# A hybrid decoder block on one core: the compression weights streamed as high and low halves, the gates' high and low columns held as one operand, and the order of all instructions set by a fixed table of urgencies

## The chip, the cores and the metric

The kernel runs on one core of one Trainium2 chip. The metric is device time in microseconds (us) for one execution, from the first to the last instruction of the program and what lies around it. The kernel before took 537.15 us, the median of three runs between 537.08 and 537.4 us.

## What is computed

One block of a decoder: x has 256 rows of 1,024 columns, and there are 256 memory rows. After an RMS norm, one wide projection `z = h @ w_in` feeds three token mixers (block-sparse attention, an mLSTM, attention to the memory), which are gated, projected, merged and normed, and a SwiGLU channel mixer ends the block. All is in float32. The change touches two small pieces of it, the compression of keys and values and the projection of the gates:

```python
def compress_blocks(kv, pe, w1, w2):
    n_cmp = (S - CMP_BLOCK) // CMP_STRIDE + 1                      # 15 blocks of 32 rows, one every 16
    idx = jnp.arange(n_cmp)[:, None] * CMP_STRIDE + jnp.arange(CMP_BLOCK)[None, :]
    blocks = kv[:, idx] + pe[None, None, :, None, :]
    hid = jax.nn.silu(jnp.einsum('bnlgd,ldh->bngh', blocks, w1))   # w1: 32 x 64 x 128, 4 groups g
    return jnp.einsum('bngh,hd->bngd', hid, w2)

z = h @ w_in[l]                                                    # 48 NSA gates and 8 mLSTM gates are columns of z
gb = jax.nn.sigmoid(g_nsa.reshape(B, S, NSA_GROUPS, NSA_HPG, 3))
gates = if_ml.astype(jnp.float32) + ml_gate_b[l].astype(jnp.float32)
logf = jax.nn.log_sigmoid(gates[..., ML_HEADS:])
```

Compression runs twice, for keys (j = 0) and for values (j = 1); its result feeds the attention scores of the first mixer.

## The kernel before

A float32 product is made of three products of a faster kind. `split` makes of a tile a high part (a rounding copy on ScalarE, type float32r) and a low part (what is left, a subtraction on VectorE), and `mm3` adds high by high, high by low and low by high in PSUM. Weights come in units of 512 KB: `fetch` loads one into `raw` (four buffers), `room` gives it a `whi` and a `wlo` (four each), and two splits fill them. `fmaj` holds weights (128x128 pieces of whi or wlo) and streams the 256 tokens; `tmaj` holds tokens and streams 512 weight columns; `fcat`, late in the kernel, holds weights and streams high and low tokens as 512 columns side by side. The tokens of the first norm are `hh` (high) and `hl` (low), 8 steps k of 128 features.

The stretch that the change touches comes early. First come the keys of the memory (`mem_k`, 96 matmuls named pd) and its values (`mem_v`, 48 matmuls named pss of 512 columns), while VectorE scales the tokens (`xt`) and makes hh and hl. `rstd_bc` works out a row's 1/rms with a power on GpSimd (`rr` for the tokens, `rm` for the memory rows) and spreads it over the partitions with two small matmuls (`rbc`). Then four units `kv` give the keys and values that are to be compressed. For each j, four ScalarE copies set up `st` (64 of 128 partitions), two VectorE copies shift it to the other 64, three GpSimd instructions clear and fill its columns for the position embedding, and 16 plain float32 matmuls hold the 128x128 pieces of `w1` and stream 80 columns of st into `ph`. Column 64 is the embedding's part and becomes the bias of the Silu that writes `hid`. The gates (`pgf`) go through `split` and `fmaj` as a unit padded to 128 columns: 24 matmuls of 256 columns. `pg` transposes them.

The order of the work is not the order of the code. Every call is recorded as an operation (Plan.record), `Plan.choose` finds an order and `Plan.issue` issues it, so that all instructions bear one line (L627). `schedule` gives each engine, in turn, the ready operation with the smallest urgency (a latest start from `latest`, less a boost), by a table of costs. `choose` tries four settings, keeps the best, and then makes 100 random trials: it raises the boost of operations in a chain that TensorE waited for, and keeps what is not longer in its own reckoning (`replay`). All engines work their queues in order; SyncE issues all loads, and a load whose buffer is still read holds up those behind it.

## Time and profile before

| what | value |
|---|---|
| median of three runs | 537.15 us |
| profiled execution, its own time | 536.95 us |
| its span, first to last instruction | 535.2 us |
| TensorE clock granted, mean | 0.996 |
| TensorE (PE) busy | 525.0 us, 3116 records |
| VectorE (DVE) busy | 411.9 us |
| ScalarE (ACT) busy | 342.2 us |
| GpSimd (POOL) busy | 30.8 us |

A busy PE is not PE at its peak: records of matmuls overlap, and a matmul's record (280 ns for 256 columns) is longer than the distance to the next start. So work on PE is counted here from start to start. A plain float32 matmul leaves two records. "Idle before" is time in which an engine had nothing running, with what ended it.

### The profile page before, as it was taken

To read this page: it belongs to the slowest core of one execution; us is meant where nothing else is said; L and a number is where in the kernel's file an instruction comes from. 1 tells how busy PE (TensorE), PEld (TensorE's weight loads), DVE (VectorE), ACT (ScalarE), POOL (GpSimd) and SP (SyncE) were. 2 spreads that over 40 slices of the span, in tenths; PEclk is the share of its full clock that TensorE was granted. 3 is DMA by queue.
4 is the path that set the end of the run, shared out by engine and by line. 5 is a ranking of instruction groups with operands and counts; after the bars stand their busy time and mean duration, and the time that the engine had idled before them with its cause. 6 is when DMAs were issued, how large, how long until landed. Compare 5 with 4: busy or idle time off the path is not lost.

```text
span 535.2 us, 8817 instructions
## 1 busy us (share of the span) xinstructions
PE 525.0 (98%) x3116; PEld 462.3 (86%) x3116; DVE 411.9 (77%) x900; ACT 342.2 (64%) x682; POOL 30.8 (6%) x43
## 2 busy tenths in 40 slices
PE   8999999999999999999999999999999999999995
PEld 8889998998989899888888888788888888888883
DVE  5786598799999988987978897966777777754543
ACT  7686787576699785966895346754665555653431
POOL 0110000020010111120220000000000000000000
PEclk9999999999999999999999999999999999999998
DMA  8995356525524454344465575734555555555512
GB/s 311 417 374 197 130 183 184 193 81 196 198 81 140 137 199 154 108 155 172 159 196 166 184 232 190 252 119 157 188 187 186 191 193 197 198 194 191 187 57 78
DMA packets 28699, 97.85 MB, mean 183 GB/s; under 512 B 3312, under 2 KB 5232, under 8 KB 28400
## 3 DMA queue, kind: packets, MB, share of 16 engines
q1 hardware_dynamic: 28656, 97.30, 52.9%
q8 instruction: 24, 0.39, 0.3%
q14 instruction: 19, 0.16, 0.1%
HBM read 95.19 MB, written 1.05 MB: 180 GB/s over the span
## 4 chain that ended last, share of the span: by engine, by line
PE 87%; DVE 5%; DMA 4%; ACT 1%; issue 1%; POOL 0%; SPq 0%; DVEq 0%; ACTq 0%
PE pd L627 47%; PE pss L627 28%; DMA raw<-in_W 4%; PE pvn L627 3%; PE sc L627 2%; PE ptn L627 2%; PE ph L627 1%; DVE wlo L627 1%; ACT whi L627 1%; DVE xt L627 1%; PE pn L627 1%; PE pvm L627 1%; PE pgf L627 1%; PE psm L627 1%; PE pq L627 1%
## 5 line engine op out<-in xcount | busy, mean ns | idle before, releaser
L627 DVE TENSOR_TENSOR wlo<-raw,whi 128x1024 fp32r<-128x1024 f32 (+1 forms) x159 | 191.8, 1213 | 80.4 <-ACT whi L627 79.9
L627 ACT ACTIVATE whi<-raw 128x1024 fp32r<-128x1024 f32 (+1 forms) x159 | 166.2, 1052 | 116.4 <-PE pd L627 57.2
L627 PE MATMUL pd<-hh,wlo 128*128 128x256 f32 x208 | 58.5, 281 | 0.0
L627 PE MATMUL pd<-hh,whi 128*128 128x256 f32 x208 | 58.4, 281 | 0.0
L627 PE MATMUL pd<-hl,whi 128*128 128x256 f32 x208 | 58.2, 280 | 0.0
L627 PE MATMUL pd<-whi,hh 128*128 128x512 f32 x144 | 57.5, 399 | 0.0
L627 PE MATMUL pd<-wlo,hh 128*128 128x512 f32 x144 | 57.5, 399 | 0.0
L627 PE MATMUL pd<-whi,hl 128*128 128x512 f32 x144 | 56.8, 398 | 0.0
L627 PE MATMUL pss<-xc,whi 128*128 128x512 f32 x168 | 43.1, 392 | 0.0
L627 PE MATMUL pss<-whi,u 128*128 128x512 f32 x132 | 42.0, 390 | 0.0
L627 PEld LDWEIGHTS pd<-hl,whi 128*128 128x128 f32 x208 | 39.3, 189 | 0.2
L627 PEld LDWEIGHTS pd<-hh,whi 128*128 128x128 f32 x208 | 39.2, 188 | 0.2
L627 PEld LDWEIGHTS pd<-hh,wlo 128*128 128x128 f32 x208 | 39.1, 188 | 0.1
L627 PEld LDWEIGHTS pss<-xc,whi 128*128 128x128 f32 x168 | 30.5, 188 | 5.2
L627 PE MATMUL pd<-xc,whi 128*128 128x512 f32 x120 | 31.9, 394 | 0.0
L627 DVE CUSTOM_DVE_ANT_0 sc<-sc,msk 128x16 f32<-128x16 f32 (+2 forms) x96 | 27.2, 313 | 5.2 <-PE sc L627 4.5
L627 PEld LDWEIGHTS pd<-whi,hh 128*128 128x128 f32 x144 | 27.1, 188 | 4.5 <-ACT cx L627 0.2
L627 PEld LDWEIGHTS pd<-whi,hl 128*128 128x128 f32 x144 | 27.1, 188 | 4.5
L627 PEld LDWEIGHTS pd<-wlo,hh 128*128 128x128 f32 x144 | 27.1, 188 | 4.0
L627 PEld LDWEIGHTS pss<-whi,u 128*128 128x128 f32 x132 | 24.8, 188 | 5.2
L627 ACT ACTIVATE pp<-sc,mx 128x128 f32<-128x128 f32 (+1 forms) x64 | 26.9, 434 | 1.8 <-DVE mx L627 1.7
L627 PE MATMUL pss<-wlo,u 128*128 128x512 f32 x66 | 25.7, 389 | 0.0
(335 smaller groups left out, 1123.3 us busy)
## 6 DMA issues: line engine op xcount, KB each, us to landing
raw<-in_W SPq DMA_DIRECT2D x161, 512.0 KB, 3.7
w<-in_w SPq DMA_DIRECT2D x2, 1024.0 KB, 7.5
xn<-in_xN SPq DMA_DIRECT2D x2, 512.0 KB, 9.4
xt<-in_xT SPq DMA_DIRECT2D x2, 512.0 KB, 9.1
mn<-in_memN SPq DMA_DIRECT2D x2, 512.0 KB, 9.3
kk<-kk SPq DMA_DIRECT2D x8, 128.0 KB, 2.8
x<-in_xN SPq DMA_DIRECT2D x2, 512.0 KB, 4.2
memt<-in_head SPq DMA_DIRECT2D x1, 512.0 KB, 7.6
```

The lines of the kernel that those rows point to most:

```text
L627: op.ins_ = getattr(op.real, op.method)(*map(arg, op.a), **{k: arg(x) for k, x in op.kw.items()})
```

## The change

- **Compression.** `st` now holds, for each of 16 steps, the high and the low parts of 64 token columns as one 128x128 held operand (column 63 is the position embedding). `w1` is split as the other weights are, high and low side by side in `w1s` (names wc in the code), and 256 columns of it are streamed: 16 float32r matmuls into `ph` [128, 2, 128] for each j. A ScalarE copy and a VectorE addition join the two halves of the columns (`hs`), one plain float32 matmul with a constant `fold` (`phT`) adds the high rows, the low rows and the embedding's rows, and Silu reads that. The GpSimd instructions for st, the shifting copies of 64 partitions and the bias are gone. ScalarE and VectorE write the two halves of st from PSUM (four each for each j), and VectorE makes the shifted half with one copy of 128 partitions.
- **Gates.** 64 gate columns are loaded, not 128; their high and low parts stand side by side in `gw`, 128 columns that are held as one operand, and high and low tokens (`hx`, one tile with hh and hl in it) are streamed as 512 columns: 8 matmuls. A copy and two additions (`gfold`) join the parts.
- **Order.** The random trials are gone. A table EARLY gives 141 of the operations a boost, in ns, by number; some costs of loads are changed, and the load of w1 stands behind the kv units in the code.

The same program text otherwise makes the instructions: all bear L621 now.

```diff
@@ -230,6 +229,9 @@
         for other in after:
             op.deps.setdefault(other, False)
         op.cost = self.cost(op)
+        if op.dma:
+            self.dmas += 1
+            op.cost *= 1.25 if self.dmas <= 6 else 1.0
...
     NEXT = {"PE": 200.0, "ACT": 135.0, "DVE": 118.0, "POOL": 80.0, "SP": 60.0}
-    START, TABLE, ISSUE, LAND = 570.0, 1283.0, 460.0, 1850.0
+    START, TABLE, ISSUE, LAND, FEED = 570.0, 1283.0, 460.0, 2100.0, 740.0
...
-        free = {e: self.START for e in self.ORDER}
+        free = {e: self.FEED if e == "SP" else self.START for e in self.ORDER}
...
-    MATMUL, SLACK, PASSES, ROUNDS = (-3.0, 0.0), (60.0, 130.0), 3, 100
+    MATMUL, SLACK, PASSES = (-3.0, 0.0), (60.0, 130.0), 3
+
+    EARLY = """
+    2:12586700 3:2093350 4:2092250 5:2093900 83:200700 145:4150 149:1400 150:4700 151:3150 152:7300 153:8600
...
+    """
 
     def choose(self):
 
@@ -554,37 +573,12 @@
         for op, op.rank in zip(self.ops, kept):
             pass
         length, matmul, slack, boost = best
-        rng = random.Random(0)
-        stale = True
-        for _ in range(self.ROUNDS):
-            if stale:
-                order = self.schedule(matmul, slack, boost)
-                self.replay(order)
-                waits = [(op.lost, op) for op in order if op.eng == "PE" and op.lost > 90 and op.why]
-                chains = []
-                for lost, op in waits:
-                    chain, d = [], op.why
-                    while d is not None and len(chain) < 16:
-                        chain.append(d.i)
...
-            if not waits:
-                break
-            chain = rng.choices(chains, [w[0] for w in waits])[0]
-            step = rng.choice((200, 500, 1000, 2000, 4000))
-            new = dict(boost)
-            for i in chain[:rng.choice((1, 2, 4, 8, 16))]:
-                new[i] = new.get(i, 0) + step
-            trial = self.replay(self.schedule(matmul, slack, new))
-            if trial <= length:
-                length, boost, stale = trial, new, True
+        boost = {int(i): int(ns) for i, ns in (x.split(":") for x in self.EARLY.split())}
         self.chosen = length, matmul, slack, boost
         return self.schedule(matmul, slack, boost)
 
     FIRST_BYTE = 0x4080
-    RESIDUE = {"vcs": 0, "V": 0, "C": 0, "G": 0, "qs": 0, "KK": 0xC0, "E": 0xC0, "Y": 0xC0, "hh": 0xC0, "hl": 0xC0,
+    RESIDUE = {"vcs": 0, "V": 0, "C": 0, "G": 0, "qs": 0, "KK": 0xC0, "E": 0xC0, "Y": 0xC0, "hh": 0xC0,
                "whi": 0, "wlo": 0, "raw": 0, "pT0": 0xC0, "pT1": 0xC0, "ce0": 0xC0, "ce1": 0xC0}
 
...
@@ -791,8 +785,8 @@
     mh = bigt("G", 3, [P, KD, S], F32R, "mh")
     ml = bigt("G", 3, [P, KD, S], F32R, "ml")
     xt = bigt("E", 2, [P, KD, S], F32, "xt")
-    hh = bigt("hh", 1, [P, KD, S], F32R, "hh")
-    hl = bigt("hl", 1, [P, KD, S], F32R, "hl")
+    hx = bigt("hh", 1, [P, 2, KD, S], F32R, "hh")
+    hh, hl = hx[:, 0], hx[:, 1]
     X, M = (hh, hl), (mh, ml)
...
-    wgt = work.tile([P, 1024], F32, tag="p", bufs=2, name="wgt")
-    w2t = work.tile([P, 192], F32, tag="ce0", bufs=1, name="w2t")
+    wgt = work.tile([P, KD, 64], F32, tag="p", bufs=2, name="wgt")
+    w2t = work.tile([P, 256], F32, tag="ce0", bufs=1, name="w2t")
...
@@ -884,13 +878,14 @@
                                      op0=ALU.mult, op1=ALU.subtract)
     fetch(("kv", 0))
     fetch(("kv", 1))
-    dma(out=wgt, in_=wg)
+    dma(out=wgt, in_=wg.rearrange("p (k n) -> p k n", k=KD))
     msk = one.tile([P, K_END - K_M0], F32, name="msk")
     w1t = [bigt("G", 3, [P, 16, P], F32, f"w1_{j}") for j in range(2)]
+    fold = w2t[:, 192:256]
     w1_in = lambda j: dma(out=w1t[j], in_=w1[j].rearrange("p (a n) -> p a n", a=16))
-    w1_in(0)
     fetch(("kv", 2))
     fetch(("kv", 3))
+    w1_in(0)
     w1_in(1)
...
@@ -907,39 +902,34 @@
 
     hid = work.tile([P, 2, NG, 32], F32, tag="ce1", bufs=1, name="hid")
     POOL.memset(hid, 0.0)
+    sts = []
     for j in range(2):
 
 
-        st = bigt("E", 2, [P, 16, 96], F32, f"st{j}")
-        POOL.memset(st[:, :, 64:96], 0.0)
-        POOL.memset(st[64:128, 15, 0:64], 0.0)
-        POOL.tensor_copy(st[:, 0:16:2, 64:66],
-                         vc[:, V_PEK + 16 * j:V_PEK + 16 * j + 16].rearrange("p (n l) -> p l n", n=2))
+        st = bigt("E", 2, [P, 2, 8, 2, 64], F32R, f"st{j}")
         ps = fpair(X, "kv", j, (ps_s, ps_d)[j])
+        by_block = lambda t: t.rearrange("p i (n q r) -> p r q i n", n=16, r=2)
         for e in range(2):
-            for i in range(2):
-                g = 2 * i + e
-                ACT.activation(st[0:64, :, 16 * g:16 * g + 16],
-                               ps[64 * e:64 * e + 64, i].rearrange("p (n l) -> p l n", n=16), AF.Copy)
-        DVE.tensor_copy(st[64:128, 0:15, 0:64], st[0:64, 1:16, 0:64])
-        DVE.tensor_copy(st[64:128, 15, 0:63], st[0:64, 0, 1:64])
-
-        ph = ps_v([P, 80], "ph")
-        for l in range(16):
-            n = l // 8
-            PE.matmul(ph, w1t[j][:, l, :], st[:, 2 * l % 16, n:n + 80], start=(l == 0), stop=(l == 15))
-        bias = work.tile([P, 1], F32, tag="b1", bufs=1, name="cbias")
-        DVE.tensor_copy(bias, ph[:, 64:65])
-        ACT.activation(hid[:, j, :, 0:NCMP], ph[:, 0:64].rearrange("p (g n) -> p g n", g=NG)[:, :, 0:NCMP], AF.Silu,
-                       bias=bias)
-
-
-    pgf = ps_s([P, S], "pgf")
-    gw = room()
-    split(gw[0], gw[1], wgt)
-    fmaj(pgf, X, range(KD), gw)
-    gts = work.tile([64, S], F32, tag="sq", bufs=3, name="gts")
-    DVE.tensor_copy(gts, pgf[0:64])
+            for r in range(2):
+                to = st[64 * r:64 * r + 64, 0].rearrange("p q x (i e n) -> p x e q i n", i=2, e=2)
+                split(to[:, 0, e], to[:, 1, e], by_block(ps[64 * e:64 * e + 64])[:, r])
+        DVE.tensor_copy(st[:, 1, :, :, 0:63], st[:, 0, :, :, 1:64].bitcast(F32))
+        pe = vc[:, V_PEK + 16 * j:V_PEK + 16 * j + 16].rearrange("p (h q) -> p h q", h=2)
+        DVE.tensor_copy(st[:, :, :, 0, 63], pe)
+        DVE.tensor_sub(st[:, :, :, 1, 63], pe, st[:, :, :, 0, 63].bitcast(F32))
+
+        sts.append(st)
+
+    pgf = ps_s([P, 2, S], "pgf")
+    gw = wpool.tile([P, 1088], F32R, tag="whi", bufs=4, name="gw")[:, 48:1072].rearrange("p (k i n) -> p k i n", k=KD, i=2)
+    split(gw[:, :, 0, :], gw[:, :, 1, :], wgt)
+    for k in range(KD):
+        PE.matmul(pgf, gw[:, k], hx[:, :, k, :], start=k == 0, stop=k == KD - 1)
+    gfold = work.tile([64, 2, S], F32, tag="sq", bufs=3, name="gfold")
+    gts = gfold[:, 0, :]
+    ACT.activation(gfold, pgf[64:128], AF.Copy)
+    DVE.tensor_add(gfold, gfold, pgf[0:64])
+    DVE.tensor_add(gts, gts, gfold[:, 1, :])
     pg = ps_s([P, 2, 64], "pg")
     for tb in range(2):
         PE.transpose(pg[:, tb, :], gts[:, tb * P:(tb + 1) * P], cs[0:64, K_ID:K_ID + 64])
@@ -957,6 +947,22 @@
     ACT.activation(lf, ef, AF.Ln, bias=1.0)
     logf = one.tile([P, 2, 4], F32, name="logf")
     DVE.scalar_tensor_tensor(logf, f, 0.0, lf, op0=ALU.min, op1=ALU.subtract)
+
+
+    for j in range(2):
+        wc = [bigt(tg, n, [P, 8, 2, P], F32R, "w1s") for tg, n in (("C", 1), ("G", 3))]
+        for h in range(2):
+            split(wc[h][:, :, 0, :], wc[h][:, :, 1, :], w1t[j][:, 8 * h:8 * h + 8, :])
+        ph = ps_v([P, 2, P], "ph")
+        for l in range(16):
+            PE.matmul(ph, sts[j][:, l // 8, l % 8].rearrange("p x n -> p (x n)"), wc[l // 8][:, l % 8],
+                      start=(l == 0), stop=(l == 15))
+        hs = work.tile([P, P], F32, tag="sq", bufs=3, name="hs")
+        ACT.activation(hs, ph[:, 1], AF.Copy)
+        DVE.tensor_add(hs, hs, ph[:, 0])
+        pc_ = ps_t([P, 64], "phT")
+        PE.matmul(pc_, hs, fold, start=True, stop=True)
+        ACT.activation(hid[:, j, :, 0:NCMP], pc_.rearrange("p (g n) -> p g n", g=NG)[:, :, 0:NCMP], AF.Silu)
...
-    yh = bigt("hh", 1, [P, 8, S], F32R, "yh")
-    yl = bigt("hl", 1, [P, 8, S], F32R, "yl")
+    yx = bigt("hh", 1, [P, 2, 8, S], F32R, "yh")
+    yh, yl = yx[:, 0], yx[:, 1]
...
-    w2 = np.concatenate([w2k, w2k, a["cmp_w2_v"][0]], axis=1)
+    fold = np.tile(np.eye(64, dtype=np.float32), (2, 1))
+    fold[63::64] = 1.0
+    w2 = np.concatenate([w2k, w2k, a["cmp_w2_v"][0], fold], axis=1)
     row = np.concatenate([a[n] for n in ("ml_head_g", "ml_gate_b", "g_post_mix", "g_post_ffn", "g_pre_ffn")], axis=1)
-    wg = np.zeros((D, P), np.float32)
+    wg = np.zeros((D, 64), np.float32)
     wg[:, 0:48] = w_in[:, C_G:C_G + 48]
     wg[:, 48:56] = w_in[:, C_IF:C_IF + 8]
-    wg = blocks(wg, slice(None)).reshape(P, 1024)
+    wg = blocks(wg, slice(None)).reshape(P, 512)
 
     cst = np.zeros((P, K_END), np.float32)
     i = np.arange(P)

```

The first 117 instructions on PE and the last 275 are the same as before, apart from names. Three places in the order, before and after, follow.

On GpSimd, from the power for the tokens' norm (rr) to what follows the power for the memory's norm (rm); before:

```order
L627 TENSOR_TENSOR rr<-rv,mhalf 128x2
L627 MEMSET st_381 128x16x32
L627 MEMSET st_381 64x64
L627 COPY st_381<-vc_358 128x8x2
L627 MEMSET st_495 128x16x32
L627 MEMSET st_495 64x64
L627 COPY st_495<-vc_358 128x8x2
L627 TENSOR_TENSOR rm<-rv,mhalf 128x2
```

And in the change:

```order
L621 TENSOR_TENSOR rr<-rv,mhalf 128x2
L621 TENSOR_TENSOR rm<-rv,mhalf 128x2
L621 MEMSET cm_799 4x128
L621 MEMSET cm_834 4x128
L621 MEMSET cx 128x2x3
```

The six instructions that set up st stood between the two powers; nothing stands there now.

On TensorE, the compression of the values before (j = 1; the rows pd around it are units of other projections, st_495 its tokens, w_1_629 its weights):

```order
L627 MATMUL pd<-hh,whi 128x256
L627 MATMUL pd<-hl,whi 128x256
L627 MATMUL ph<-st_495,w_1_629 128x80 x16
L627 MATMUL pg<-cs,gts 128x64 x2
L627 MATMUL pd<-hh,wlo 128x256
```

And the compression of the keys in the change (st_565; the name hh now stands for high and low tokens alike, since they are one tile):

```order
L621 MATMUL pd<-hh,whi 128x256
L621 MATMUL ph<-w1s,st_565 128x256 x8
L621 MATMUL pd<-hh,whi 128x256
L621 MATMUL ph<-w1s,st_565 128x256 x4
L621 MATMUL pg<-cs,gfold 128x64 x2
L621 MATMUL ph<-w1s,st_565 128x256 x4
L621 MATMUL psm<-kmem,qm_731 128x256 x4
```

The 16 matmuls are no longer one block, and the transposes of the gates stand among them; 49 matmuls of projections stand between pgf and the first ph now, where 11 to 12 stood on either side of pgf before.

On VectorE, the rows before from the split of the gate weights to the gates' copy:

```order
L627 TENSOR_TENSOR wlo<-wgt,whi 128x1024
L627 COPY st_381<-st_381 64x63
L627 TENSOR_TENSOR wlo<-raw,whi 128x1024 x2
L627 COPY cbias<-ph 128x1
L627 COPY st_495<-st_495 64x15x64
L627 COPY gts<-pgf 64x256
```

And in the change from the last projection unit ahead of the splits of w1 to the second pair of them:

```order
L621 TENSOR_TENSOR wlo<-raw,whi 128x1024
L621 TENSOR_TENSOR st_637<-pd,st_637 64x8x2x16 x4
L621 TENSOR_TENSOR gfold<-gfold,pgf 64x512
L621 CAST st_637<-st_637 128x16x63
L621 TENSOR_TENSOR w1s<-w_0_580,w1s 128x8x128 x2
L621 TENSOR_TENSOR gfold<-gfold 64x256
L621 CAST st_637<-vc 128x16
L621 TENSOR_TENSOR wlo<-raw,whi 128x1024
L621 TENSOR_TENSOR st_637<-vc,st_637 128x16
L621 TENSOR_TENSOR wlo<-raw,whi 128x1024
L621 TENSOR_TENSOR hs<-hs,ph 128x128
L621 TENSOR_TENSOR w1s<-w_1_647,w1s 128x8x128 x2
```

The subtractions for st and for w1 stand among the low parts of the weight units (wlo) on which the projections' matmuls wait.

More of the change, by code (lines that the diff above doesn't have):

```diff
@@ L2 @@
 import math
-import random
 from contextlib import ExitStack, contextmanager
@@ L176, in __init__ @@
         nc = tc.nc
-        self.tc, self.ops, self.tiles, self.boost = tc, [], {}, 0
+        self.tc, self.ops, self.tiles, self.boost, self.dmas = tc, [], {}, 0, 0
         self.engines = {n: Engine(self, n, e) for n, e in
@@ L471, in replay @@
     def replay(self, order):
-        free = {e: self.START for e in self.ORDER}
+        free = {e: self.FEED if e == "SP" else self.START for e in self.ORDER}
         place, port, busy, done = {}, {}, {}, {}
@@ L556, in choose @@
         length, matmul, slack, boost = best
-        rng = random.Random(0)
-        stale = True
-        for _ in range(self.ROUNDS):
-            if stale:
-                order = self.schedule(matmul, slack, boost)
-                self.replay(order)
-                waits = [(op.lost, op) for op in order if op.eng == "PE" and op.lost > 90 and op.why]
-                chains = []
-                for lost, op in waits:
-                    chain, d = [], op.why
-                    while d is not None and len(chain) < 16:
-                        chain.append(d.i)
-                        d = d.why or max((x for x, strict in d.deps.items() if strict), key=lambda x: x.end,
-                                         default=None)
-                    chains.append(chain)
-                stale = False
-            if not waits:
-                break
-            chain = rng.choices(chains, [w[0] for w in waits])[0]
-            step = rng.choice((200, 500, 1000, 2000, 4000))
-            new = dict(boost)
-            for i in chain[:rng.choice((1, 2, 4, 8, 16))]:
-                new[i] = new.get(i, 0) + step
-            trial = self.replay(self.schedule(matmul, slack, new))
-            if trial <= length:
-                length, boost, stale = trial, new, True
+        boost = {int(i): int(ns) for i, ns in (x.split(":") for x in self.EARLY.split())}
         self.chosen = length, matmul, slack, boost
```

13 rows, old and new, of the table EARLY are left out of this document.

## Prediction

> **What bounds the kernel now.** I read first the page's busy times, then who waited for whom, then the timeline of each engine in the stretch of the change, then the sums by stretch.
>
> ```profile
> PE 525.0 (98%) x3116; PEld 462.3 (86%) x3116; DVE 411.9 (77%) x900; ACT 342.2 (64%) x682; POOL 30.8 (6%) x43
> PE rbc L627 <- POOL rm L627: 1.3, 1, 1.3
> PE warm L627 <- POOL mhalf L627: 1.0, 1, 1.0
> PE pd L627 <- ACT whi L627: 0.8, 1, 0.8
> PE pss L627 <- ACT xc L627: 0.2, 1, 0.2
> ```
>
> TensorE is busy 98% of the span and waits 3.3 us in all, so the span is the sum of its matmuls, a start and a tail. The reader should see two things. First, whatever shortens TensorE's own work shortens the kernel by as much, provided nobody else comes late. Second, one wait, 1.3 us for GpSimd's `rm`, lies in the stretch of the change. So the question has two halves: how much TensorE work goes, and whether VectorE, which takes over work, can keep up.
>
> ```profile
> 30.00:40.00 10.00, 8.70 (x74) 8.50 (x73) 7.77 (x13) 7.38 (x14) 2.48 (x4) 1.00 0.94 356
> 40.00:45.00 5.00, 5.00 (x46) 5.00 (x45) 4.91 (x6) 3.56 (x5) 0.87 (x2) 1.00 0.54 200
> 45.00:60.00 15.00, 15.00 (x133) 14.85 (x132) 5.08 (x13) 10.06 (x15) 0.00 (x0) 1.00 0.48 165
> 60.00:65.00 5.00, 5.00 (x47) 5.00 (x46) 3.86 (x7) 3.96 (x6) 0.00 (x0) 1.00 0.28 101
> 65.00:80.00 15.00, 15.00 (x133) 14.82 (x132) 14.89 (x38) 11.71 (x27) 0.00 (x0) 1.00 0.56 188
> ```
>
> The columns are PE, PEld, DVE, ACT and POOL busy. VectorE has room from 45 to 60 us (5.08 of 15 busy) and none from 65 to 80 (14.89 of 15); TensorE nevertheless did not wait there, because what it ran was ready earlier.
>
> **The compression's matmuls.** These rows are TensorE's timeline; work is counted from start to start.
>
> ```profile
> 36.61 0.28 PE L627 MATMUL pd<-hh,whi 128*128 128x256 f32 x1
> 40.74 0.28 PE L627 MATMUL pd<-hh,wlo 128*128 128x256 f32 x1
> 40.86 3.69 PE L627 MATMUL ph<-st,w 128*128 128x80 f32 x32
> 44.34 0.36 PE L627 MATMUL pd<-hh,whi 128*128 128x256 f32 x1
> 45.80 0.28 PE L627 MATMUL pgf<-hh,whi 128*128 128x256 f32 x1
> 48.52 0.28 PE L627 MATMUL pd<-hh,whi 128*128 128x256 f32 x1
> 49.77 3.69 PE L627 MATMUL ph<-st,w 128*128 128x80 f32 x32
> 53.39 0.33 PE L627 MATMUL pg<-cs,gts 64*128 64x64 f32 x2
> 77.08 1.00 PE L627 MATMUL pvc<-w2t,hrep 128*128 128x64 f32 x8
> 77.92 0.61 PE L627 MATMUL ptx<-cs,pp 128*128 128x128 f32 x4
> ```
>
> The two blocks ph took 44.34 - 40.86 = 3.48 and 53.39 - 49.77 = 3.62 us: 7.10 us go. What comes is 32 float32r matmuls of 256 columns. Such matmuls run at 0.118 us each (35 steps from 36.61 to 40.74) or at 0.113 (pgf: 24 from 45.80 to 48.52). I take 0.113 here and a term for the slower pace below: 32 x 0.113 = 3.62. The two plain float32 fold matmuls of 64 columns cost what a pvc does, (77.92 - 77.08) / 4 = 0.21: 0.42. Net: -7.10 + 3.62 + 0.42 = **-3.06 us**.
>
> **The gates.** 24 matmuls took 48.52 - 45.80 = 2.72 us. For 8 of 512 columns the nearest rows are those of the memory's values:
>
> ```profile
> 17.81 0.40 PE L627 MATMUL pss<-wlo,mh 128*128 128x512 f32 x1
> 20.10 0.39 PE L627 MATMUL pss<-whi,ml 128*128 128x512 f32 x1
> ```
>
> Ten steps in 2.29 us are 0.229 each, so 8 cost 1.83: **-0.89 us**. The new operand streams two pieces of 256 columns that lie apart, where these rows stream one piece; I see no row for that and allow 0 to 0.3 us, taking 0. [...]
>
> **The wait for rm.** These rows are the powers and their neighbours on GpSimd, then VectorE, then TensorE around the wait.
>
> ```profile
> 18.95 0.20 POOL L627 COPY st<-vc 128x16 f32<-128x16 f32 x1 [0.24 <-DMA vc<-in_vec]
> 30.57 0.73 POOL L627 MEMSET st<- 128x512 f32 x2 [11.42 <-DVE hl L627]
> 31.37 1.15 POOL L627 COPY st<-vc 128x16 f32<-128x16 f32 x1
> 32.48 0.69 POOL L627 TENSOR_TENSOR rm<-rv,mhalf 128x2 f32<-128x2 f32 x1
> 30.43 0.16 DVE L627 TENSOR_SCALAR rv<-sums 128x2 f32<-128x2 f32 x1
> 31.24 1.23 DVE L627 TENSOR_TENSOR wlo<-raw,whi 128x1024 fp32r<-128x1024 f32 x1 [0.65 <-ACT whi L627]
> 31.65 0.28 PE L627 MATMUL pss<-hh,wlo 128*128 128x256 f32 x1
> 33.23 0.49 PE L627 MATMUL rbc<-cs,rm 128*128 128x128 f32 x2 [1.30 <-POOL rm L627]
> ```
>
> The sums for rm were ready at 30.59 (30.43 + 0.16). GpSimd, in its queue's order, was still to clear and fill st1, whose buffer came free only with the last hl; the power ran from 32.48 to 33.17, and rbc started at 33.23, where without a wait it would have started at 31.65 + 0.12 = 31.77. That is 1.46 us. The change takes these three instructions out of the queue: the power can start right after its sums and, with its own 0.69 us, end at about 31.3 on before's clock, ahead of the 31.77 at which TensorE wants it. **-1.46 us**; nothing later in GpSimd's queue is due soon. What would be late next is VectorE's wlo of the following unit, below.
>
> **A slower pace.** In this trace the 256-column matmuls ran at 0.118 us before the first ph and at 0.113 after it. I don't know what sets it. If taking the plain float32 block away leaves the slow pace until 78 us, some 200 matmuls lose 0.005 each: 1.0 us. The small float32 matmuls (pg, phT, pf) that stay could end it as well. I take **+0.3**, ends 0 and 1.0.
>
> **VectorE's added work.** Durations by groups:
>
> ```profile
> L627 DVE TENSOR_TENSOR wlo<-raw,whi 128x1024 fp32r<-128x1024 f32 x155 | 189.2, 1226 | 79.4 <-ACT whi L627 78.9
> L627 DVE TENSOR_TENSOR hl<-xt,hh 128x256 fp32r<-128x256 f32 x8 | 2.9, 418 | 0.0
> L627 DVE TENSOR_TENSOR kt<-pd,rmb 128x512 f32<-128x512 f32 x2 | 1.4, 684 | 0.0
> L627 DVE COPY st<-st 64x960 f32<-64x960 f32 x2 | 1.4, 684 | 2.2 <-ACT st L627 2.2
> L627 DVE TENSOR_SCALAR mx<-mx 128x2 f32<-128x2 f32 x4 | 0.6, 148 | 0.0
> L627 DVE COPY gts<-pgf 64x256 f32<-64x256 f32 x1 | 0.4, 417 | 0.7 <-PE pgf L627 0.7
> ```
>
> Added: four low parts of w1 at 1.23 (4.9); eight low parts of st, 256 wide from PSUM, at 0.42 (3.3); two shifting copies at about 0.7 (1.4); four small ones at 0.15 (0.6); gfold at 0.68 and 0.42 (1.1); hs twice at about 0.3 (0.6); gw, 512 wide, 0.7. Sum 12.6. Removed: the copies of st, two of 0.68 and two of about 0.2 (1.8), wgt's low part (1.2), gts (0.4), two biases (0.3): 3.7. Net +8.9 us. Room for it between 30 and 65 us: 35 less 7.77 + 4.91 + 5.08 + 3.86 = 21.6 busy leaves 13.4 us idle; but TensorE now crosses that stretch 3.06 + 0.89 + 1.46 = 5.4 us sooner, so 8.0 are left. 8.9 against 8.0: 0.9 us too little, in front of a stretch (65 to 80) where VectorE is full. I expect it to show where TensorE reaches small matmuls that hang on VectorE's chain (`pm` behind the running maxima `cm`, the transposes `ptx`): **+0.9 us**, ends 0 (projections run ahead instead, as they did before at 65 to 80) and 2.5. ScalarE's share, some 5 us (four high parts of w1, gw, gfold, hs), fits into 45 to 65, where it was busy 10.06 + 3.96 of 20 us.
>
> **Moved things at nothing.** The tokens' rbc stands 12 matmuls later, and scaling xt and making hh and hl is then done in one run; from there to the first matmul that needs hh are 24 x 0.229 = 5.5 us, while VectorE's 16 instructions of that size (hl: 0.42) make 6.7 us, and the eighth step is needed only 7 x 0.35 = 2.5 us after the first. If that cover fails it costs what is short, up to 1 us. A unit is loaded ahead of the rows for the norms on SyncE's queue; it has the same margin. `hid` is ready later, by a copy, an addition and the fold, but its first reader stands just ahead of pvc, at about 75 us. Elsewhere the order differs in many places, but the waits above leave little to win or lose outside the stretch: 0, ends -0.8 and +0.8.
>
> **The sum.** -3.06 - 0.89 - 1.46 + 0.3 + 0.9 = -4.2 us. The profiled execution took 536.95, so 532.7 there; against the median of 537.15, which stands 0.2 higher, 532.9. That is the forecast.
>
> **The rivals.** (1) The wait for rm stays, behind another lock. The copy of 16 elements took 0.20 us at 18.95 but 1.15 at 31.37, and it ended at 32.52, just after VectorE's subtraction from two SBUF tiles (31.24 to 32.47). If the power comes when such a subtraction is under way, it stands still until that ends: the power is then done as late as before, at 33.17, and the 1.46 us stay: 534.4. In before the sums led the next subtraction by 0.65 us idle, which speaks against; in the change ScalarE's order still puts the unit's high part behind the sums. Chance 0.2. [...]
>
> (2) VectorE becomes the bound. If none of its idle time can be used, because the splits are tied to the arrival of units and to four buffers, all 8.9 us land on TensorE's path: -5.4 + 0.3 + 8.9 = +3.8, that is 541, slower. For it speaks that VectorE is full from 65 to 80; against it that its 10 us of idle time at 45 to 60 lie just where the new work becomes ready. It is slower than before by 0.2% once over 6.2 us stay uncovered. Chance 0.04 for that, and 0.08 for a half of it, which is no change that can be told (-0.6).
>
> (3) All of the new work is covered, the fast pace holds and the new order saves some of the rest: -5.4 - 0.8 gives 530.9. Chance 0.2.
>
> (4) Nothing is won on the matmuls: the new ones run as plain float32 in two passes. The 128-column rows at 77.92 and the block ph show such passes at about 0.11 us per 80 columns, so 32 of 256 columns would take over 10 us more. The operands are float32r like those of pd; chance 0.01.
>
> **How the numbers follow.** The forecast has 0.47. A measurement of this kernel can tell about 0.2%, 1.1 us. The range reaches from case 3, 530.9, to 535.2: the sum with 2.5 for VectorE and 0.7 for the pace or the lock. Faster by over 0.2% (below 536.1): the forecast, (1) and (3), 0.87; within it: the half of (2), 0.08; slower: the rest of (2) and (4), 0.05.
>
> **What would show it.** After: the span near 531; 16 ph in two or three pieces at 0.113 to 0.118; pgf 8 in 1.8 us; no wait of rbc on rm; GpSimd's power at 0.7 us directly behind rv; VectorE nearly full from 30 to 80; TensorE's new waits, if any, on cm, nm or ptx. It is wrong if ph comes as two records each, if the waits of TensorE grow by more than 2.5 us, or if the time is lost outside the first 85 us.

## The result, and the profile after

| | before | after |
|---|---|---|
| median, four runs each | 537.25 us (537.08 to 537.4) | 532.46 us (531.99 to 533.01) |
| ratio | 1 | 0.9911, 95% interval [0.9894, 0.9929] |
| profiled execution, its own time | 536.95 us | 531.99 us |
| its span | 535.2 us | 529.9 us |

The change is 4.8 us faster; 4.2 were forecast. First, as for before, the busy times on the page of after, and TensorE's waits (all but that of the first matmul on mhalf).

```profile
PE 521.3 (98%) x3072; PEld 458.0 (86%) x3072; DVE 418.5 (79%) x915; ACT 348.2 (66%) x689; POOL 25.4 (5%) x37
```

```profile
...
PE pd L621 <- ACT whi L621: 0.8, 1, 0.8
PE ptx L621 <- DVE xg L621: 0.3, 1, 0.3
PE pss L621 <- DVE xc L621: 0.3, 1, 0.3
```

The wait of rbc on rm is gone, and two waits of 0.3 us came far behind the stretch of the change, at 337 and 340 us. TensorE is as full as before, and VectorE is busy 6.6 us more (418.5 for 411.9). Next, two of the stretches shown of before; columns PE, PEld, DVE, ACT and POOL.

```profile
45.00:60.00 15.00, 15.00 (x129) 14.80 (x129) 13.87 (x23) 12.35 (x19) 0.39 (x2) 1.00 0.48 168
...
65.00:80.00 15.00, 15.00 (x120) 14.32 (x120) 14.75 (x39) 13.87 (x36) 0.00 (x0) 1.00 0.46 151
```

VectorE went from 5.08 to 13.87 of 15 us at 45 to 60: the idle time there is used up. TensorE has no idle time in either row. Its timeline shows the new matmuls, again counted from start to start.

```profile
40.73 2.00 PE L621 MATMUL pgf<-hh,gw 128*128 128x512 f32 x8
42.57 0.40 PE L621 MATMUL pd<-hh,whi 128*128 128x256 f32 x2
...
48.35 1.11 PE L621 MATMUL ph<-w1s,st 128*128 128x256 f32 x8
49.29 0.28 PE L621 MATMUL pd<-hh,whi 128*128 128x256 f32 x1
49.41 0.63 PE L621 MATMUL ph<-w1s,st 128*128 128x256 f32 x4
49.98 0.33 PE L621 MATMUL pg<-cs,gfold 64*128 64x64 f32 x2
50.24 0.74 PE L621 MATMUL ph<-w1s,st 128*128 128x256 f32 x4
50.81 0.64 PE L621 MATMUL psm<-kmem,qm 128*128 128x256 f32 x4
...
53.97 1.07 PE L621 MATMUL ph<-w1s,st 128*128 128x256 f32 x8
54.88 0.28 PE L621 MATMUL pd<-hh,wlo 128*128 128x256 f32 x1
...
55.12 1.11 PE L621 MATMUL ph<-w1s,st 128*128 128x256 f32 x8
56.06 0.29 PE L621 MATMUL pd<-hh,whi 128*128 128x256 f32 x1
```

pgf took 42.57 - 40.73 = 1.84 us. The five pieces of ph took 0.94 + 0.57 + 0.57 + 0.91 + 0.94 = 3.93; the phT rows add 0.30 (four starts in all, summed over the trace). GpSimd's power with VectorE's rows around it, then TensorE around rbc:

```profile
30.25 0.17 DVE L621 TENSOR_SCALAR rv<-sums 128x2 f32<-128x2 f32 x1
31.12 1.23 DVE L621 TENSOR_TENSOR wlo<-raw,whi 128x1024 fp32r<-128x1024 f32 x1 [0.71 <-ACT whi L621]
30.49 0.70 POOL L621 TENSOR_TENSOR rm<-rv,mhalf 128x2 f32<-128x2 f32 x1 [10.63 <-DVE rv L621]
```

```profile
31.70 0.28 PE L621 MATMUL pss<-hh,wlo 128*128 128x256 f32 x1
31.82 0.61 PE L621 MATMUL rbc<-cs,rm 128*128 128x128 f32 x4
```

The power starts 0.07 us behind its sums and ends at 31.19 (31.3 was forecast); rbc follows its neighbour after 0.12 us, without a wait.

The whole span, all starts of TensorE summed by kind: ph with phT -2.87, pgf -0.88, the wait for rm -1.46, rbc's own steps -0.10, the other 256-column matmuls -0.52, the 128-column ones +0.74, the 512-column ones +0.26, the rest +0.05, and the tail behind the last matmul's start -0.50 (7.08 to 6.58). That is -5.28, and the spans differ by 535.2 - 529.9 = 5.3. Two of these terms are sums of parts with opposite causes far behind the stretch: the +0.74 are two kinds of transposes (ptn +0.41, ptm +0.33), and the -0.52 contains -0.77 of sc, the attention scores.

The tail shows at VectorE's last instructions, before and then after.

```profile
530.10 1.54 DVE L627 SCALAR_TENSOR_TENSOR z<-z,ss,x 128x512 f32<-128x512 f32 x3
525.33 1.54 DVE L621 SCALAR_TENSOR_TENSOR z<-z,ss,x 128x256 f32<-128x256 f32 x3
```

They end 3.5 us before the end of the span in before and 3.0 in after. So the 0.5 us lies behind all computing.

### The profile page after: what moved, and what is told of

Same layout as the page of the kernel before. It is cut to its first block, busy times and chain, and to the rows that moved or that the text cites. A ratio compares the mean times of both kernels' runs of the same rounds, so it can differ in the third digit from the quotient of the medians.

```text
span 529.9 us, 8725 instructions
## 1 busy us (share of the span) xinstructions
PE 521.3 (98%) x3072; PEld 458.0 (86%) x3072; DVE 418.5 (79%) x915; ACT 348.2 (66%) x689; POOL 25.4 (5%) x37
## 4 chain that ended last, share of the span: by engine, by line
PE 93%; DVE 2%; DMA 2%; issue 1%; ACT 1%; SPq 0%; DVEq 0%
PE pd L621 50%; PE pss L621 30%; PE pvn L621 3%; PE sc L621 2%; PE ptn L621 2%; DMA raw<-in_W 2%; PE ph L621 1%; PE pn L621 1%; PE pvm L621 1%; PE psm L621 1%; DVE wlo L621 1%; DVE wq L621 1%; DVE z L621 0%; PE ptx L621 0%; PE pq L621 0%
## 5 line engine op out<-in xcount | busy, mean ns | idle before, releaser
L621 DVE TENSOR_TENSOR wlo<-raw,whi 128x1024 fp32r<-128x1024 f32 (+1 forms) x159 | 191.8, 1211 | 77.1 <-ACT whi L621 76.5
L621 ACT ACTIVATE whi<-raw 128x1024 fp32r<-128x1024 f32 (+1 forms) x159 | 166.5, 1052 | 100.6 <-PE pd L621 48.8
L621 PE MATMUL pd<-whi,hh 128*128 128x512 f32 x288 | 96.1, 398 | 0.0
L621 PE MATMUL pd<-hh,whi 128*128 128x256 f32 x416 | 75.0, 280 | 0.0
L621 PEld LDWEIGHTS pd<-hh,whi 128*128 128x128 f32 x416 | 64.1, 189 | 0.4
L621 PEld LDWEIGHTS pd<-whi,hh 128*128 128x128 f32 x288 | 53.0, 188 | 8.5
L621 PE MATMUL pd<-hh,wlo 128*128 128x256 f32 x208 | 58.6, 282 | 0.0
L621 PE MATMUL pd<-wlo,hh 128*128 128x512 f32 x144 | 57.4, 399 | 0.0
L621 PE MATMUL pss<-xc,whi 128*128 128x512 f32 x168 | 43.4, 393 | 0.0
L621 PE MATMUL pss<-whi,u 128*128 128x512 f32 x132 | 42.0, 390 | 0.0
L621 PEld LDWEIGHTS pd<-hh,wlo 128*128 128x128 f32 x208 | 39.1, 188 | 0.2 <-DVE wlo L621 0.2
L621 PEld LDWEIGHTS pss<-xc,whi 128*128 128x128 f32 x168 | 30.6, 188 | 5.3
L621 PE MATMUL pd<-xc,whi 128*128 128x512 f32 x120 | 31.8, 395 | 0.0
L621 PEld LDWEIGHTS pd<-wlo,hh 128*128 128x128 f32 x144 | 27.1, 188 | 4.1
L621 DVE CUSTOM_DVE_ANT_0 sc<-sc,msk 128x128 f32<-128x128 f32 (+2 forms) x96 | 27.1, 316 | 2.9 <-PE sc L621 2.4
L621 PEld LDWEIGHTS pss<-whi,u 128*128 128x128 f32 x132 | 24.8, 188 | 5.2
L621 ACT ACTIVATE pp<-sc,mx 128x128 f32<-128x128 f32 (+1 forms) x64 | 26.6, 428 | 0.5 <-DVE mx L621 0.5
L621 PE MATMUL pss<-wlo,u 128*128 128x512 f32 x66 | 25.7, 389 | 0.0
L621 PEld LDWEIGHTS pd<-xc,whi 128*128 128x128 f32 x120 | 22.0, 188 | 3.8
L621 PEld LDWEIGHTS pss<-xc,wlo 128*128 128x128 f32 x168 | 22.4, 188 | 1.7
L621 PE MATMUL pss<-xc,wlo 128*128 128x256 f32 x168 | 22.8, 278 | 0.0
L621 DVE TENSOR_SCALAR pp<-pp,sm 128x256 f32<-128x256 f32 (+1 forms) x72 | 19.6, 316 | 0.0
```

Of the source, the lines that this page charges most:

```text
L621: op.ins_ = getattr(op.real, op.method)(*map(arg, op.a), **{k: arg(x) for k, x in op.kw.items()})
```

## The experiments

Two theories were tested. Mine: the gain is TensorE's work that went (-3.06 and -0.89) and a wait behind GpSimd's queue (-1.46), little of it given back. The rival: the gain belongs to the table of urgencies, without which VectorE's added work would eat it. Of the first, each term was tried alone; of the second, the table was taken out. All ratios are against the kernel before on the same chip, whose medians were 536.6 to 536.7 us there.

**GpSimd's three instructions moved behind rm, in before.**

```diff
         order = self.choose()
+        name = lambda op: op.outs[0].tile.name if op.eng == "POOL" else ""
+        moved = [op for op in order if name(op) == "st1"]
...
+        order = [op for op in order if op not in moved]
+        at = [name(op) for op in order].index("rm") + 1
+        order[at:at] = moved
```

> The kernel before, its own order, with one move: GpSimd's three instructions on st1 (two memsets and the copy from vc) stand behind the power rm and no longer ahead of it. Nothing else is changed. Theory (the wait of rbc on rm is GpSimd's queue and lies on the path): the power starts near 30.6 us and not at 32.48, the 1.3 us wait of rbc goes, and the time falls by 1.2 to 1.5, to about 535.8 us. Rival (the wait only changes its cause, to VectorE or to another operand): the time stays at 537.2, within 0.4.

Measured: 536.11 us for 536.63, ratio 0.9991 [0.9982, 0.9999], 0.5 us less. GpSimd's and TensorE's timelines of this run:

```profile
29.91 0.70 POOL L633 TENSOR_TENSOR rm<-rv,mhalf 128x2 f32<-128x2 f32 x1 [10.37 <-DVE rv L633]
30.56 0.73 POOL L633 MEMSET st<- 128x512 f32 x2
```

```profile
31.66 0.28 PE L633 MATMUL pss<-hh,wlo 128*128 128x256 f32 x1
31.78 0.61 PE L633 MATMUL rbc<-cs,rm 128*128 128x128 f32 x4
...
32.47 0.28 PE L633 MATMUL pss<-hh,wlo 128*128 128x256 f32 x1
33.60 0.28 PE L633 MATMUL pss<-hh,whi 128*128 128x256 f32 x1
```

The mechanism is as forecast: the power comes first, and the wait is gone, with no other wait of rbc in its place. So the rival's cause falls. Its time (no change, within 0.4) does not quite, and my size does: 1.2 to 1.5 was expected, and 0.05 to 1.0 is what the interval leaves.

**Before once more, for a second profiled execution.** No edit.

> The kernel before once more, for a second profiled execution. In the first, GpSimd's copy of 16 columns in front of rm took 1.15 us and rbc waited 1.30 us; taking the three instructions away brought 0.52 us in the medians. Theory A (the wait is 1.2 to 1.4 us in every execution): rbc waits 1.2 to 1.4 us again. Theory B (GpSimd's durations differ from execution to execution, and the first profile was a bad one): the copy takes 0.2 to 0.8 us and rbc waits 0.3 to 1.0 us.

Measured: 536.39 us for 536.72, ratio 0.9995 [0.9986, 1.0005]. GpSimd and TensorE:

```profile
29.78 0.73 POOL L627 MEMSET st<- 128x512 f32 x2 [9.94 <-DMA raw<-in_W]
30.58 1.16 POOL L627 COPY st<-vc 128x16 f32<-128x16 f32 x1
```

```profile
31.95 0.28 PE L627 MATMUL pss<-hh,wlo 128*128 128x256 f32 x1
32.45 0.71 PE L627 MATMUL rbc<-cs,rm 128*128 128x128 f32 x4 [0.21 <-POOL rm L627]
```

The wait was 0.21 us, not 1.30, and not for theory B's reason: the copy took 1.16 again. GpSimd's three instructions began 0.79 us earlier (29.78 for 30.57), and TensorE reached rbc 0.30 us later (the matmul ahead of it began at 31.95 for 31.65; its first pd had begun at 5.10, in the first profile at 4.60). The wait is the outcome of a race between two chains that began at different times in the two executions. So the 1.46 us of one trace was a single draw. What the run with the moved instructions gained in its medians, 0.5, is the better size for this term.

**Three GpSimd instructions put ahead of rm, in after.**

```diff
+                if op.eng == "POOL" and op.outs[0].tile.name == "rm":
+                    big, small = self.extra
+                    op.real.memset(big.real()[:, 0:2, :], 0.0)
+                    op.real.memset(big.real()[64:128, 2, 0:64], 0.0)
+                    op.real.tensor_copy(big.real()[:, 3, 0:16], small.real()[:, V_PEK:V_PEK + 16])
...
+    plan.extra = xt, vc
```

> The kernel after, its own order, with three GpSimd instructions put ahead of the power rm that do what those of before did there (two memsets and a copy of 16 columns from vc, onto xt, whose values nobody reads any more). Theory: they start when the last low part of hh is written, rm ends 1.9 us later, rbc waits 1.3 to 1.5 us for it, and the time rises by as much, to about 533.9 us. Rival (the wait of before was one of its order, and the table of urgencies covers such a delay): the time stays at 532.5, within 0.4.

Measured: 532.15 us, ratio 0.9915 [0.9902, 0.9928]: no cost that can be told (its tail is 0.36 us longer than after's, see the next section). It tells nothing for or against the theory, because the three instructions did not wait as those of before did: the part of xt that they cleared was free early, and in the trace they were done at 31.70 us, when the sums for rm were just there (31.76). It serves instead as a second sample of after's order. With the part of xt that is read last:

```diff
-                    op.real.memset(big.real()[:, 0:2, :], 0.0)
-                    op.real.memset(big.real()[64:128, 2, 0:64], 0.0)
-                    op.real.tensor_copy(big.real()[:, 3, 0:16], small.real()[:, V_PEK:V_PEK + 16])
+                    op.real.memset(big.real()[:, 6:8, :], 0.0)
+                    op.real.memset(big.real()[64:128, 7, 0:64], 0.0)
+                    op.real.tensor_copy(big.real()[:, 7, 64:80], small.real()[:, V_PEK:V_PEK + 16])
```

> The run with three GpSimd instructions ahead of rm, mended: the first of them now clears the part of xt that the last two low parts of hh read, so that all three start only when the last low part is written, as those of before did; in the first version they ran 1.2 us before rv was there and cost nothing. Theory (what stands in GpSimd's queue behind a late operand holds rm, and TensorE behind it): rm ends 1.1 to 1.7 us later than in after, rbc waits 0.6 to 1.4 us, and the time is 0.6 to 1.4 above the 532.15 of the first version, 532.8 to 533.6 us. Rival (it is covered): 532.2 to 532.5 and no wait of rbc on rm.

Measured: 533.49 us, ratio 0.993 [0.9916, 0.9943], 0.8 us above the other by the ratios and 1.3 by the medians. GpSimd and VectorE, then TensorE:

```profile
31.32 1.23 DVE L626 TENSOR_TENSOR wlo<-raw,whi 128x1024 fp32r<-128x1024 f32 x1 [0.71 <-ACT whi L626]
31.39 1.21 POOL L625 COPY xt<-vc 128x16 f32<-128x16 f32 x1
32.56 0.70 POOL L626 TENSOR_TENSOR rm<-rv,mhalf 128x2 f32<-128x2 f32 x1
```

```profile
33.31 0.71 PE L626 MATMUL rbc<-cs,rm 128*128 128x128 f32 x4 [1.23 <-POOL rm L626]
```

The wait is back, in another kernel and another order, put there by nothing but three instructions in GpSimd's queue. The theory holds: the wait (1.23 us) and the time were in the range expected, though rm ended at 33.26, 2.1 us later than in after, where 1.1 to 1.7 was expected. The times themselves stand in two groups, 532.22 twice and 533.45 to 533.63 three times, as a race between two chains would have it; only one of the five was traced.

**Half of the compression's products left out, in after.**

```diff
+        self.products = {}
...
+                if op.eng == "PE" and op.outs[0].tile.name == "ph" and not op.kw["start"]:
+                    done = self.products[op.outs[0].tile] = self.products.get(op.outs[0].tile, 0) + 1
+                    if done > 7:
+                        continue
+                    op.kw["stop"] = done == 7
```

> The kernel after, its own order, with half of the compression's products left out: of the 16 matmuls ph of keys and of values only the first 8 are issued, so the compressed keys and values lack the other half of their sum; all splits, folds and loads stay. Theory (TensorE sets the end in this stage, and the gain of the change is the matmul time that went): 16 x 0.113 to 0.118 = 1.8 to 1.9 us less, to about 530.6 us. Rival (VectorE is what the stage waits for, and products come out of its shade): no change, 532.5, within 0.4.

Measured: 531.05 us, ratio 0.9899 [0.9886, 0.9912], that is 1.1 us below the run with after's order on the same chip (532.15). Between the same two kernels, the starts of TensorE in the profiled executions sum to 2.0 us less, all of it in ph (3.94 to 1.89). But 0.36 us of the 1.1 is the other run's longer tail (6.94 for 6.58), and with four and five runs that scatter over 1.5 us each, the medians can't tell what is left from 1.9, nor safely from nothing. What speaks against the rival is the trace: the matmul time went, and no new wait over 0.3 us took its place.

**VectorE's four low parts of w1 computed twice, in after.**

```diff
                 op.ins_ = getattr(op.real, op.method)(*map(arg, op.a), **{k: arg(x) for k, x in op.kw.items()})
+                if op.eng == "DVE" and op.outs[0].tile.name == "w1s":
+                    op.ins_ = getattr(op.real, op.method)(*map(arg, op.a), **{k: arg(x) for k, x in op.kw.items()})
```

> The kernel after, its own order, with each of VectorE's four low parts w1s computed twice over: four more subtractions of 128 x 1024, 1.2 us each, 4.9 us more work for VectorE between 44 and 62 us. What the prediction held (VectorE has no room left there; what exceeds 8.0 us shows in full): 4 to 5 us slower, about 537 us. What the trace of after suggests (it is idle 1.1 us in 45 to 60, 1.0 in 60 to 65, 4.5 in 80 to 100, and TensorE waited 0.3 for it): part of it shows, 1 to 3 us, 533.5 to 535.5. Rival (VectorE's work is covered, since what follows is due much later): no change, 532.5, within 0.4.

Measured: 536.34 us, ratio 0.9993 [0.9984, 1.0002]: about 4 us slower than after. TensorE's longest wait, and its timeline around the first ph:

```profile
PE ph L621 <- DVE w1s L623: 1.9, 2, 1.1
```

```profile
49.49 1.21 PE L621 MATMUL ph<-w1s,st 128*128 128x256 f32 x8 [0.83 <-DVE w1s L623]
...
51.89 0.90 PE L621 MATMUL ph<-w1s,st 128*128 128x256 f32 x4 [1.07 <-DVE w1s L623]
```

There is no room left on VectorE for 4.9 us more, as the prediction held; reading the room from its idle time (1.1 us in 45 to 60) would have been too hopeful. The doubled subtractions are also the very ones that ph waits for, so this measures how late w1s may come as much as how full VectorE is. Part of the price is the clock: 1.0 us went in ten matmuls at half speed behind the idle time (rows in the last section).

**The planner's order without trials or table: before, its two halves, after.** Four kernels on one chip. In the first, before's hundred trials are set to none. The second adds the gates' part of the change to it, the third the compression's part (with w1's load behind the kv units). The fourth is after with an empty table.

```diff
-    MATMUL, SLACK, PASSES, ROUNDS = (-3.0, 0.0), (60.0, 130.0), 3, 100
+    MATMUL, SLACK, PASSES, ROUNDS = (-3.0, 0.0), (60.0, 130.0), 3, 0
```

```diff
-        boost = {int(i): int(ns) for i, ns in (x.split(":") for x in self.EARLY.split())}
```

> The kernel before without its hundred random trials: the order is that of the planner's latest starts alone. It is the base for the two halves of the change that are put on it next, so that none of them has trials or a table of its own. Theory: the trials took small waits of TensorE away, some 1 to 3 us in all, so 538 to 540 us. Rival (the trials are worth nothing): 537.2, within 0.4.

> The planner's plain order, and of the change only the gates: 64 columns, high and low held as one operand, hh and hl in one tile, 8 matmuls of 512 columns for 24 of 256, and the fold; no trials and no table. Theory (matmul time is what the change takes away): 0.9 us less than the plain before (24 x 0.113 - 8 x 0.229). Rival (the gain sits in the order that the table gives): no difference to the plain before beyond what another order scatters, 0.5.

> The planner's plain order, and of the change only the compression: states and w1 held as high and low parts, 32 matmuls of 256 columns for 32 plain F32 ones, folds, w1_in behind the fetch of kv 3; no trials and no table. Theory: 7.1 - 3.6 - 0.4 = 3.1 us less than the plain before by the matmuls, and up to 1.5 more where the plain order too has st1's instructions ahead of rm: 3.1 to 4.6 less, offset by up to 1 where VectorE's 8 us more are not covered without a table. Rival (without the table VectorE's added work eats it): no faster than the plain before.

> The kernel after with its table of urgencies emptied: the order is that of the planner's latest starts alone. Theory (the table replaces the trials and brings little of its own; the gain is work that went): about 4 us less than the plain before, by the same gates and compression, and 1 to 3 us slower than after, 533.5 to 535.5. Rival (the gain is the table's): the plain after stands within 1 us of the plain before, and 4 or more above after.

| planner's plain order | median us | ratio to before, 95% interval |
|---|---|---|
| before | 538.99 | 1.0040 [1.0028, 1.0053] |
| gates alone | 537.83 | 1.0023 [1.0014, 1.0032] |
| compression alone | 537.58 | 1.0016 [1.0007, 1.0025] |
| after | 541.0 | 1.0080 [1.0067, 1.0094] |

The gates give 0.9 us by the ratios (1.2 by the medians) where 0.9 was expected. The compression gives 1.3 to 1.4 where 3.1 to 4.6 was expected, less up to 1 for VectorE. And both together, on the new planner constants, are 2.0 us slower than the plain before, where I had expected 4 faster. After's TensorE waits in this order:

```profile
PE pss L620 <- DVE wlo L620: 1.8, 3, 1.0
PE pvn L620 <- POOL ce L620: 1.2, 3, 0.4
PE pd L620 <- DVE wlo L620: 1.1, 2, 0.6
```

The matmul time is gone here too: against the plain before, ph with phT took 3.0 us less and pgf 0.9 in the trace. But the 512-column matmuls took 4.6 us more and the 256-column ones 1.6, from waits for VectorE and GpSimd, most of them outside the stretch of the change. On this point the rival is right.

**After with the hundred trials of before in place of the table, and after with an empty table and before's planner constants.**

```diff
-        boost = {int(i): int(ns) for i, ns in (x.split(":") for x in self.EARLY.split())}
+        rng = random.Random(0)
+        for _ in range(self.ROUNDS):
...
```

> The kernel after with the table taken out and the hundred random trials of before put back in its place; the new planner constants stay. The plain order stood at 541.0 us, after with its table at 532.5, and on before the trials were worth 2.3 us (538.99 to 536.72). Theory A (an order found by trials is as good as the table): 532 to 534 us. Theory B (the trials bring here what they brought on before, and the gain over before hangs on the table): 541.0 - 2.3 = 538.7, 537.5 to 539.5 us, slower than before.

```diff
-            op.cost *= 1.25 if self.dmas <= 6 else 1.0
+            op.cost *= 1.0
...
-    START, TABLE, ISSUE, LAND, FEED = 570.0, 1283.0, 460.0, 2100.0, 740.0
+    START, TABLE, ISSUE, LAND, FEED = 570.0, 1283.0, 460.0, 1850.0, 570.0
...
-        boost = {int(i): int(ns) for i, ns in (x.split(":") for x in self.EARLY.split())}
```

> The kernel after with an empty table and with the planner constants of before too (landing 1850, SP's start 570, no surcharge on the first six loads). Theory A (the plain order is poor because VectorE's added work and the changed steps find no good places, whatever the constants): 541, 540 to 542 us. Theory B (the new constants spoil the plain order, and the two halves of the change add up under the old ones): 538.99 - 1.16 - 1.41 = 536.4, 535.5 to 537.5 us.

Measured: with trials 538.33 us, ratio 1.0031 [1.0019, 1.0043]; with the old constants 541.15 us, 1.0081 [1.0067, 1.0096]. Theory B holds for the first, theory A for the second: the constants do nothing, and the trials bring 2.7 us, which leaves the change slower than before. Against the 532.46 and 532.15 of after's own order, the table is worth about 6 us more than the trials. One place shows where. VectorE at 20 to 30 us, first in after, then in after with trials:

```profile
20.78 3.69 DVE L621 TENSOR_TENSOR wlo<-raw,whi 128x1024 fp32r<-128x1024 f32 x3 [1.78 <-ACT whi L621]
24.39 3.22 DVE L621 SCALAR_TENSOR_TENSOR xt<-xt,vc,rbc 128x256 f32<-128x256 f32 x8
```

```profile
21.71 1.26 DVE L647 SCALAR_TENSOR_TENSOR xt<-xt,vc,rbc 128x256 f32<-128x256 f32 x3 [2.08 <-PE rbc L647]
...
23.62 1.23 DVE L647 TENSOR_TENSOR wlo<-raw,whi 128x1024 fp32r<-128x1024 f32 x1
...
27.67 1.22 DVE L647 TENSOR_TENSOR wlo<-raw,whi 128x1024 fp32r<-128x1024 f32 x1
```

TensorE with trials waited for just those two:

```profile
24.91 0.50 PE L647 MATMUL pss<-wlo,mh 128*128 128x512 f32 x1 [0.53 <-DVE wlo L647]
28.95 0.50 PE L647 MATMUL pss<-wlo,mh 128*128 128x512 f32 x1 [1.02 <-DVE wlo L647]
```

The table lets VectorE finish three low parts of the memory's value units before it scales the tokens. The trials' order scales tokens first and brings the low parts when TensorE already stands before them. These two waits are 1.5 of the 6 us; the rest is spread over other places.

No run gives the kernel before a table of its own. An estimate from its trace bounds what that could win: of the 3.3 us that TensorE waited, the first two waits (1.0 on mhalf and 0.8 on whi) stand in after too, which leaves about 1.5 us, small stops left aside, where the change won 4.8.

## Why the prediction came out right, and what in it was wrong

The sum came out right (532.9 forecast, 532.46 measured) with two terms that held, two that were too large with opposite signs, one that was missing, and a premise that was true only because of the table. The two matmul terms, 3.9 of the 4.2 us, were understood; that the rest came out so close is in part luck, because about 1 us too much for rm stood against 0.9 too much for VectorE and a tail that was not forecast.

- **The compression's matmuls, -3.06: right.** It is -2.87 in the trace. The 3.62 for 32 matmuls came out at 3.93, of which 0.2 went at the two steps beside pg (0.57 for four matmuls) and 0.1 by the slower pace; the folds took 0.30 where 0.42 was set down.
- **The gates, -0.89: right.** -0.88; the two pieces of the streamed operand cost nothing (1.84 us for the eight, where 1.83 was set down). The plain order with the gates alone gave the same 0.9.
- **The wait for rm, -1.46: right mechanism, wrong size.** The prediction took it from one execution. A second one of the same kernel waited 0.21, and taking the cause away alone brought 0.5 us. The term should have been a range from near 0 to 1.5. Rival (1), that VectorE's subtractions would hold the power as long, did not happen: the power took 0.70 us and was over, at 31.19, 0.07 us after the next subtraction had begun (31.12). What the rival read from the copy of 16 elements was seen again: the copy took 1.15 us in before, 1.16 in its second execution and 1.21 in the second run with GpSimd's instructions put ahead of rm, and each time it ended 0.05 or 0.06 us behind VectorE's subtraction (at 32.52, 31.74 and 32.60, with the subtraction at 32.47, 31.68 and 32.55); at 18.95 in before, with VectorE idle, it had taken 0.20. But the power came in the gap in front of the subtraction, so whether one holds a power too is not shown.
- **VectorE's added work, +0.9: nothing of it shows in the trace.** Before pm, cm or ptx of the stretch, where I expected it, nothing was lost. The one new stop of TensorE in the stretch has another cause. These are TensorE and its weight loads in after:

```profile
35.01 0.39 PE L621 MATMUL pd<-hh,whi 128*128 128x256 f32 x2
35.40 0.19 PEld L621 LDWEIGHTS pd<-hh,wlo 128*128 128x128 f32 x1 [0.20 <-DVE wlo L621]
35.40 0.39 PE L621 MATMUL pd<-hh,wlo 128*128 128x256 f32 x1
35.62 0.40 PE L621 MATMUL pd<-hh,whi 128*128 128x256 f32 x2
```

  Two steps that take 0.23 elsewhere took 0.39, and the next 0.22: 0.27 us in all, for a late wlo. But VectorE's first added instruction (the low parts of st) starts only at 37.66. It is a price of the order: here VectorE makes both kt ahead of that wlo (32.92 to 34.21), in before only one, and the run with GpSimd's instructions moved, which has before's order and reached this place as early, did not stop there. The prediction named this wlo as what would be late next and set nothing down for it. The step that failed is the comparison of 8.9 us of new work with 8.0 us of room. By the durations of the records the 8.9 was right (all of VectorE's records together are 9.2 us longer). But records on VectorE overlap, so that its busy time, the measure in which the room was taken, rose by 6.6 only. In the same measure the work fits into the room.
- **The pace, +0.3: right size, wrong picture.** Of the steps between 256-column matmuls, 558 ran at 0.115 us or less and 571 above it (up to 0.121) before, 491 and 645 after: +0.33 us. But the pace does not hang on the plain float32 block (last section).
- **Missing: the tail, -0.5.** The forecast had no term for it, and it belongs to the change. From the last matmul's start to the end, the traces of all kernels with the six GpSimd instructions for st take 7.05 to 7.08 us, those of all kernels without them 6.58 or 6.59 (the compression alone in the plain order too, at 6.59; the gates alone 7.05), and the two with three such instructions put back 6.91 and 6.94. In all of them VectorE ends (at 3.55 us) and the last output lands (at 5.70) equally far behind that matmul; the difference is a pause at GpSimd's closing instructions: ahead of its last drain it stood still for 0.37 us in before and 0.03 in after, and that drain took 0.17 us and 0.04. Why the pause depends on what GpSimd had to do before is not shown.
- **"The waits above leave little to win or lose outside the stretch: 0": true of these two kernels, wrong as a reason.** The order is what keeps that term at 0, and as a sum of parts that cancel: behind 99 us, sc takes 0.8 us less in after, ptn and ptm 0.74 more, and both come back to within 0.2 us in the other traces of the two orders. With the planner's plain order, the same instructions lose more than the 3.9 us that the matmuls save; with the trials of before the change ends 0.3% slower. A 0.05 for slower was fair only because the order that after runs could be read instruction by instruction; for the change without its table it would have been wrong.

## What to carry to other kernels

Where an engine is 98% busy, count the work that goes from it start to start, and that part of a forecast will hold (here -2.87 and -0.88 us came of -3.06 and -0.89); but a wait read from a single execution is one draw of a race between chains (rbc waited 1.30 us in one execution of before and 0.21 in the next), and its size needs a second execution. Added work and the idle time that is to take it up have to be counted in the same measure, because records overlap (on VectorE 9.2 us more by the records, 6.6 by the busy time). When work moves from the full engine to one that is nearly as full, the old order or the old search may no longer be good enough: here the same instructions were 0.9% faster or 0.3% slower than before by their order alone.

## What the hardware showed beside

**Half the clock after short idle times.** In after with the plain order, and then in after with the low parts doubled (columns as above, the first figure behind POOL is the granted clock):

```profile
116.00:120.30 4.30, 3.29 (x17) 2.30 (x16) 4.01 (x14) 2.31 (x8) 1.29 (x3) 0.98 0.00 0
120.30:123.30 3.00, 3.00 (x9) 2.21 (x7) 3.00 (x5) 0.17 (x1) 0.00 (x0) 0.50 0.76 238
```

```profile
50.50:53.20 2.70, 1.63 (x10) 1.09 (x8) 2.67 (x5) 1.06 (x1) 0.00 (x0) 0.83 0.00 0
53.20:55.60 2.40, 2.40 (x11) 2.40 (x12) 2.31 (x5) 1.22 (x3) 0.00 (x0) 0.50 0.53 148
```

TensorE was busy 3.29 of 4.30 us, and 1.63 of 2.70; then it got half its clock (0.50 for 3.00 us, and for 2.40) although it was busy all the time, and a 512-column matmul took 0.43 us for 0.23. So behind waits of 0.4 to 1.1 us up to 1.4 us more went. Both stretches were only partly idle (1.01 us of 4.30, 1.07 of 2.70). Not every such stretch has the half clock behind it: before's wait of 1.30 us for rm lies in a stretch (30 to 40 us, 8.70 busy) whose granted clock was 1.00, as in the next (40 to 45). What brings the half clock, and how much idle time it takes, is not shown.

**The two paces.** In the run with GpSimd's instructions moved, the steps behind rbc took (33.60 - 32.47) / 10 = 0.113 us, in before, at the same place of the same order, 0.118. So neither the order nor a block of plain float32 matmuls sets the pace. It changes where other matmuls stand between, at rbc in that run, at ph in before, but not each time: in before it stayed at 0.118 across rbc. What decides it stays open.
